# Two encoder layers in split float32: the gate and half of the output projection multiply high and low parts as one product of 512 columns

## The chip, the cores and the metric

The kernel runs on one core of a Trainium2 chip. TensorE (PE) multiplies, VectorE (DVE), ScalarE (ACT) and GpSimd (POOL) work beside it, SyncE (SP) issues loads. Times are device microseconds of the whole execution, the median of the runs. A profile is one execution recorded by the hardware; its span runs from the first to the last instruction of the program.

## The reference

Two layers over 256 positions of width 2048. Each layer is RMSNorm, an input projection into a convolution group and an attention group with their gates, an output projection with residual, and a gated embedding:

```python
for i in range(DEPTH):                       # 2
    hn = _rmsnorm(h, norm_g[i])
    u = hn @ w_in[i]                         # 2048 -> 5632 columns
    ...                                      # ya: convolution group, yb: attention group, 1024 each
    h = h + jnp.concatenate([ya, yb], axis=-1) @ w_out[i]     # 2048 -> 2048
    e = _rmsnorm(p[i] @ w_pe[i], pe_g[i])
    h = h + e * jax.nn.sigmoid(h @ w_pg[i])                   # 2048 -> 2048
return _rmsnorm(h, final_g)
```

Everything is float32.

## The kernel before

Activations lie with the width on the 128 partitions and the 256 positions along the free dimension, so a 2048-wide operand is 16 rows of tiles, 128 x 256 each. A float32 product is made of three products in a reduced type (float32r): each operand is split into a high part (a cast) and a low part (the value less its high part), and `mm3` (lines 398 to 403) sums high x high (L401), high weights x low operand (L402) and low weights x high operand (L403) in one PSUM bank. One such group of three, for one tile of 128 rows, is called a **step** here.

**Weights** come as a stream of **halves** of 128 x 1024, which is eight tiles of 128 x 128, in the order of their use; 156 halves are one layer. Two halves are one load of 1 MB on SP's queue, three loads deep. `split` (L163) casts a half to its high part on ACT (L168) and subtracts on DVE for the low part (L171), into one of five buffers `w`. `get` emits, before the products of half h, the split of half h + 4. The cast of that half waits until TensorE is through with half h - 1, which had the buffer. Engines work strictly in the order in which the code emits, each in its own queue.

**Operands** are tiles of 128 x 2 x 8 x 256: first the eight high parts of eight rows, then the eight low parts. `bigt` makes them: `hg` (the normed input), `ya` and `yb` (what the two groups hand to the output projection), `h1` (the sum after it, the gate's operand).

**The stretch around the change**, with a layer's halves counted from 0:

- Halves 92 to 107: first half of the output projection, over `yb`, summed into `az`. The convolution group's LayerNorm runs beside it on DVE and ACT.
- Halves 108 to 123: its second half, over `ya`. Two output tiles share a PSUM bank `o`; behind a pair stands one add of 512 columns into `az` (DVE, L778), a cast to `h1`'s high part (ACT, L779), and the subtraction for its low part (DVE, L780), which `later` puts behind the next half's products.
- Halves 124 to 155: the gate, two halves to a tile, two tiles to a pair and a bank `g`. The first pair takes rows 0 to 7 of both tiles first and then rows 8 to 15, so that `h1`'s last rows are needed in the third gate half. `gate` does the rest of a pair: sum of `h1`'s parts (DVE, L799), sigmoid (ACT, L801), product and sum (DVE, L803, L804), square (ACT, L391) for the next norm. The last two tiles are single, with 256 columns in `gate`. In the second layer ACT also scales the results (L817). Beside the first 14 gate halves DVE norms the embedding, one L540 to a half.

Of the kernel before, what the change touches and what calls it, by code (L numbers as in the profile page):

```python
# [10 lines left out]
F32 = mybir.dt.float32  # L11
F32R = mybir.dt.float32r
# [5 lines left out]
P = 128  # L18
# [30 lines left out]

NB_FIRST = KT  # L50
NSPL = 5
SHIFT = 16
MAN = 'DVE,PE,Activation'
LY = (2, 2)
ORD = 1
# [74 lines left out]
def trunk_kernel(ctx: ExitStack, tc: tile.TileContext, xT, pT, wst, par, gain, relb, sinkp, onehot, out):  # L130
# [12 lines left out]
    def bigt(name, dt=F32):  # L143

        return big.tile([P, 2, 8, S], dt, tag="big", name=name)

    def halves(t):
        return [t[:, 0], t[:, 1]]

    def bank(name):  # L150
        return ps.tile([P, 2, S], F32, tag="ps", name=name)
# [11 lines left out]
    def split(h):  # L163
        raw = raws[h // 2][:, h % 2, :]
        w = wspl.tile([P, 2 * HALF + 64], F32R, tag="w", name=f"w{h}")
        w = w[:, SHIFT:SHIFT + 2 * HALF].rearrange("p (t n) -> p t n", t=2)
        hi, lo = w[:, 0], w[:, 1]
        nc.scalar.copy(hi, raw)  # L168
        spl[h] = w
        if h not in (4, 5):  # L170
            nc.vector.tensor_sub(lo, raw, hi.bitcast(F32))  # L171

    def first_lo(h):

        w = spl[h]
        nc.vector.tensor_sub(w[:, 1], raws[h // 2][:, h % 2, :], w[:, 0].bitcast(F32))

    def ahead(h):

# [218 lines left out]
    def mm3(o, w, x, start, stop):  # L398


        nc.tensor.matmul(o, w[:, 0], x[:, 0], start=start, stop=False, skip_group_check=True)  # L401
        nc.tensor.matmul(o, w[:, 0], x[:, 1], start=False, stop=False, skip_group_check=True)  # L402
        nc.tensor.matmul(o, w[:, 1], x[:, 0], start=False, stop=stop, skip_group_check=True)  # L403

    class Cursor:
        h = 0
# [1 line left out]
    def step(o, X, start, stop):  # L408

        steps([o], X, [start], stop)  # L410

    def steps(os, X, starts, stop):

        parts = []
        for _ in os:
            name, _, k0, nk = HALVES[Cursor.h % NHALF]
            parts.append(get(Cursor.h).rearrange("p t (k c) -> p t k c", k=nk))
            Cursor.h += 1
        for kk in range(nk):
            k = k0 + kk  # L420
            for o, w, start in zip(os, parts, starts):
                mm3(o, w[:, :, kk, :], X[k // 8][:, :, k % 8, :], start and kk == 0, stop and kk == nk - 1)
# [16 lines left out]
    for l in range(DEPTH):  # L439
# [7 lines left out]
        def operand(k, l=l, h=h, hg=hg):  # L447

            i, kk = k // 8, k % 8
            if kk == 0:  # L450
                hg.append(bigt(f"hg{l}_{i}", F32R))
# [20 lines left out]
        for q in range(4):  # L472
            n = Cursor.h
            Cursor.h += 1
            if l:
                w = get(n).rearrange("p t (j k c) -> p t j k c", j=4, k=2)
            else:
                raw = raws[n // 2][:, n % 2, :].rearrange("p (j k c) -> p j k c", j=4, k=2)
            for jj in range(0, 4, 2):
                j = 4 * q + jj  # L480
                b = bank("e")
                for x in range(2):
                    for k in range(2):
                        if l:
                            mm3(b[:, x, :], w[:, :, jj + x, k, :], pp[:, :, k, :], x == 0 and k == 0, k == 1)
                        else:
                            nc.tensor.matmul(b[:, x, :], raw[:, jj + x, k, :], pf[:, k, :], start=x == 0 and k == 0,
                                             stop=k == 1, skip_group_check=True)
                if l == 0 and j // 2 < 4:
                    for k in (4 * (j // 2), 4 * (j // 2) + 2):  # L490
                        if k < KT - 2:
                            square_acc(hacc, h[k // 8][:, k % 8:k % 8 + 2, :], k == 0, nc.vector)
                    if j // 2 == 3:
                        sq = wk.tile([P, 2, S], F32, name="sq", tag="sq", bufs=3)
                        nc.scalar.activation(sq, h[1][:, 6:8, :], AF.Square)
                        hparts = halves_of(sq) + [fold(hacc)]
                if j // 2 == QQ[l][0]:
                    dg = rstd_col(hparts, D, f"rh{l}")
                    ahead(5 if l == 0 else Cursor.h - 1 - q + 5)
                if j // 2 == QQ[l][1]:  # L500
                    rbs.append(rstd_row(dg, f"rh{l}", copy=False))
                    if l == 0:
                        first_lo(4)
                        operands(0, 1)
                        first_lo(5)
                        subs.pop(0)()
                        operands(2, 1)
                if QQ[l][1] + (l == 0) <= j // 2 <= QQ[l][1] + 1:
                    operands(4 * (j // 2 - QQ[l][1]), 2)
                ecopy.append((j, b))  # L510

                while ecopy and 4 * (l == 0) <= j // 2 < 6:
                    copied(*ecopy.pop(0))
            pump()
# [89 lines left out]
        for q in range(4):  # L604
            n = Cursor.h
            Cursor.h += 1
            w = get(n).rearrange("p t (k c) -> p t k c", k=4)
            for kk in range(4):
                k = 4 * q + kk
                for b in range(2):  # L610
                    mm3(vb[b][:, 0, :], hg[k // 8][:, :, k % 8, b * P:(b + 1) * P], w[:, :, kk, :],
                        k == 0, k == KT - 1)
            pump()
        v = wk.tile([P, 2, W_KV], F32, name=f"v{l}", tag="v", bufs=1)
        for b in range(2):
# [85 lines left out]
        for t in range(0, NCT, 2):  # L701
            b = pair(hg, f"za{l}_{t}")
            if t == NCT - 2:
                finish(l)

                for k in (0, 4):
                    nc.gpsimd.dma_start(a[:, k:k + 4, :], hsrc[:, k:k + 4, :])
                yb = bigt(f"yb{l}", F32R)
# [3 lines left out]
        ya = bigt(f"ya{l}", F32R)  # L712

        def lnorm(l=l, acc=acc, za=za, ya=ya, ysum=ysum, done=done):

# [54 lines left out]
        for j in range(0, KT, 2):  # L770
            d = az[:, j // 8, j % 8:j % 8 + 2, :]
            if j % 8 == 0:
                h1.append(bigt(f"h1{l}_{j // 8}", F32R))
# [4 lines left out]
            nc.vector.tensor_add(d, b, d)  # L778
            nc.scalar.copy(hi, d)  # L779
            sub = lambda d=d, hi=hi, lo=lo: nc.vector.tensor_sub(lo, d, hi.bitcast(F32))  # L780
            if j < KT - 2:
                later(sub)
            else:
                sub()
# [40 lines left out]
        hparts = []  # L825
        for j in range(0, KT - 2, 2):
            if j:
                b = pair(h1, f"g{l}_{j}")
            else:
                b = bank(f"g{l}_{j}")  # L830
                for n in range(2):
                    for x in range(2):
                        step(b[:, x, :], h1, n == 0 and x == 0, n == 1)
            gate(j, b)
            if j == 4 and not last:
                pp = wk.tile([P, 4 * S + 32], F32R, name="pp", tag="qq")
                pp = pp[:, 24:24 + 4 * S].rearrange("p (x k s) -> p x k s", x=2, k=2)
                hilo(pp[:, 0], pp[:, 1], pf)
        for j in range(KT - 2, KT):
            b = bank(f"g{l}_{j}")[:, 0:1, :]  # L840
            for n in range(2):
                step(b[:, 0, :], h1, n == 0, n == 1)
            gate(j, b)
        drain()
        h = e

# [92 lines left out]
```

## Time and profile before

| | us |
|---|---|
| median of 3 runs | 937.89 (937.57 to 939.52) |
| the profiled execution | 937.63 |
| its span | 935.9 |
| weight casts on ACT, 308 | 315.5 busy |
| weight subtractions on DVE, 306 | 374.1 busy |
| adds of 512 behind the second half of the output projection, 16 | 11.0 busy |

The granted TensorE clock is 0.997 of full speed over the span. A row of the groups reads: line, engine, operation, output and inputs by the program's names, shapes, count, then busy time and mean ns of one, then the idle time ahead of them and what ended it. In a timeline the first number is the start in us from the span's start, the second the duration; successive products overlap, so their distance is read from the starts.

### The profile page before, as it was taken

Reading aid. Unit: us, or ns where it says so; the run is one execution under the profiler, and the core shown is the slowest. Engines: PE = TensorE matmul, PEld = TensorE weight load, DVE = VectorE, ACT = ScalarE, POOL = GpSimd, SP = SyncE. Lnnn points to the kernel's source line nnn. Section 1 sums busy time; section 2 is a strip of 40 time slices with the busy share of each in tenths; the row PEclk is TensorE's granted clock in tenths of the full one; section 3 lists DMA queues with packets and bytes.
Section 4 is the critical chain, followed back from the end, with each engine's and each line's share of the span. In section 5 each row is a group of like instructions: output and inputs, shape, how many; then the busy total and the mean of one; then the engine's idle time right before and its main releaser. Section 6 shows DMA issues by size and latency. Waiting matters only on the chain.

```text
span 935.9 us, 19124 instructions
## 1 busy us (share of the span) xinstructions
PE 923.6 (99%) x7968; PEld 910.3 (97%) x7968; DVE 767.6 (82%) x1282; ACT 548.9 (59%) x830; POOL 82.4 (9%) x79
## 2 busy tenths in 40 slices
PE   8999999999999999999999999999999999999995
PEld 7999999999999999999999999999999999999995
DVE  4999999998887686786679999999888877777663
ACT  4655454788874555554467444569788546445551
POOL 0022001010000000011102100000100000000111
PEclk9999999999999999999999999999999999999998
DMA  8674556555547456556656556465555564655532
GB/s 301 232 251 158 203 180 239 184 198 187 183 162 257 164 203 218 182 181 238 210 183 203 180 203 226 171 214 196 187 169 181 182 208 154 244 183 181 202 111 91
DMA packets 29011, 182.55 MB, mean 195 GB/s; under 512 B 3595, under 2 KB 4156, under 8 KB 9084
## 3 DMA queue, kind: packets, MB, share of 16 engines
q1 hardware_dynamic: 24284, 165.70, 50.6%
q0 software_dynamic: 3344, 12.88, 4.3%
q10 hardware_dynamic: 1296, 2.75, 0.8%
q8 instruction: 62, 1.02, 0.4%
q14 instruction: 25, 0.20, 0.1%
HBM read 177.09 MB, written 4.23 MB: 194 GB/s over the span
## 4 chain that ended last, share of the span: by engine, by line
PE 95%; DVE 2%; DMA 1%; ACT 1%; issue 0%; POOL 0%; ACTq 0%; DVEq 0%
PE ag L401 6%; PE ag L402 6%; PE ag L403 6%; PE o L401 6%; PE o L402 6%; PE o L403 6%; PE g L403 6%; PE g L402 6%; PE g L401 6%; PE za L401 3%; PE za L403 3%; PE za L402 3%; PE zb L403 3%; PE zb L401 3%; PE zb L402 3%; PE q L401 3%
## 5 line engine op out<-in xcount | busy, mean ns | idle before, releaser
L171 DVE TENSOR_TENSOR w<-raw,w 128x1024 fp32r<-128x1024 f32 x306 | 374.1, 1231 | 100.0 <-ACT w L168 99.0
L168 ACT CAST w<-raw 128x1024 fp32r<-128x1024 f32 x308 | 315.5, 1046 | 160.1 <-PE ag L403 44.0
L565 DVE SCALAR_TENSOR_TENSOR cz<-az,pars,cz 128x241 f32<-128x241 f32 (+11 forms) x480 | 216.7, 500 | 1.0
L401 PE MATMUL ag<-hg,w 128*128 128x256 f32 x512 | 142.2, 278 | 0.0
L402 PE MATMUL ag<-hg,w 128*128 128x256 f32 x512 | 141.8, 277 | 0.0
L403 PE MATMUL ag<-hg,w 128*128 128x256 f32 x512 | 141.8, 277 | 0.0
L403 PE MATMUL g<-h,w 128*128 128x256 f32 x512 | 141.3, 276 | 0.0
L401 PE MATMUL g<-h,w 128*128 128x256 f32 x512 | 141.3, 276 | 0.0
L402 PE MATMUL g<-h,w 128*128 128x256 f32 x512 | 141.3, 276 | 0.0
L401 PEld LDWEIGHTS ag<-hg,w 128*128 128x128 f32 x512 | 96.1, 188 | 0.9 <-ACT w L168 0.8
L402 PEld LDWEIGHTS ag<-hg,w 128*128 128x128 f32 x512 | 96.4, 188 | 0.1
L403 PEld LDWEIGHTS ag<-hg,w 128*128 128x128 f32 x512 | 96.1, 188 | 0.0
L401 PEld LDWEIGHTS g<-h,w 128*128 128x128 f32 x512 | 96.1, 188 | 0.0
L402 PEld LDWEIGHTS g<-h,w 128*128 128x128 f32 x512 | 96.1, 188 | 0.0
L403 PEld LDWEIGHTS g<-h,w 128*128 128x128 f32 x512 | 96.1, 188 | 0.0
L401 PE MATMUL za<-hg,w 128*128 128x256 f32 x256 | 71.7, 280 | 0.0
L401 PE MATMUL o<-yb,w 128*128 128x256 f32 x256 | 71.4, 279 | 0.0
L401 PE MATMUL q<-hg,w 128*128 128x256 f32 x256 | 71.4, 279 | 0.0
L401 PE MATMUL zb<-hg,w 128*128 128x256 f32 x256 | 71.3, 279 | 0.0
L403 PE MATMUL zb<-hg,w 128*128 128x256 f32 x256 | 71.0, 277 | 0.0
L402 PE MATMUL zb<-hg,w 128*128 128x256 f32 x256 | 71.0, 277 | 0.0
L403 PE MATMUL za<-hg,w 128*128 128x256 f32 x256 | 71.0, 277 | 0.0
(227 smaller groups left out, 2264.0 us busy)
## 6 DMA issues: line engine op xcount, KB each, us to landing
raw<-in_wst SPq DMA_DIRECT2D x153, 1024.0 KB, 4.9
bias<-fscr POOLq DMA_DIRECT2D x16, 384.0 KB, 3.9
raw<-in_wst SPq DMA_DIRECT2D x4, 512.0 KB, 8.1
az<-in_xT POOLq DMA_DIRECT2D x4, 512.0 KB, 5.6
hscr<-e POOLq DMA_DIRECT2D x2, 1024.0 KB, 5.7
az<-hscr POOLq DMA_DIRECT2D x4, 512.0 KB, 6.0
x<-in_xT SPq DMA_DIRECT2D x3, 512.0 KB, 8.4
out_t<-og ACTq DMA_DIRECT2D x4, 256.0 KB, 3.0
```

The source lines that it names most:

```text
L168: nc.scalar.copy(hi, raw)
L171: nc.vector.tensor_sub(lo, raw, hi.bitcast(F32))
L401: nc.tensor.matmul(o, w[:, 0], x[:, 0], start=start, stop=False, skip_group_check=True)
L402: nc.tensor.matmul(o, w[:, 0], x[:, 1], start=False, stop=False, skip_group_check=True)
L403: nc.tensor.matmul(o, w[:, 1], x[:, 0], start=False, stop=stop, skip_group_check=True)
L565: nc.vector.scalar_tensor_tensor(acc[:, t, lo_:hi_], a[:, t, lo_ + s:hi_ + s], w(k), acc[:, t, lo_:hi_], ALU.mult, ALU.add)
```

## The change

Operands lie as 128 x 8 x 2 x 256 now (`operand_tile`): the high and the low part of a row side by side, 512 columns in one piece; views keep the old index order. In the weight buffers the low part begins 32 elements further on (20 from half 108 on), and `split` hands out the two parts instead of one tile.

`mm3` has two forms. Where the output has three dimensions, high weights multiply the 512 columns of high and low operand in one product, and low weights multiply the high part into the second 256 columns. A whole PSUM bank then belongs to one tile, and its two halves are summed afterwards. All other uses keep three products (`prod3`). The wide form is used in the second half of the output projection, and in the gate but for the last tile of the second layer.

In the output projection each tile has its own bank and two adds of 256 columns into `az`. In the gate `merge` copies each tile's second 256 columns to SBUF on ACT and adds the first 256 on DVE; the sigmoid reads that sum.

```diff
+    def operand_tile(name):
+        t = big.tile([P, 8, 2, S], F32R, tag="big", name=name)
+        return t.rearrange("p k t s -> p t k s")
...
     def mm3(o, w, x, start, stop):
-        nc.tensor.matmul(o, w[:, 0], x[:, 0], start=start, stop=False, skip_group_check=True)
-        nc.tensor.matmul(o, w[:, 0], x[:, 1], start=False, stop=False, skip_group_check=True)
-        nc.tensor.matmul(o, w[:, 1], x[:, 0], start=False, stop=stop, skip_group_check=True)
+        if len(o.shape) == 3:
+            nc.tensor.matmul(o, w[0], x, start=start, stop=False, skip_group_check=True)
+            nc.tensor.matmul(o[:, 1], w[1], x[:, 0], start=False, stop=stop, skip_group_check=True)
+            return
+        prod3(o, w, parts_of(x), start, stop)
...
+    def merge(bs):
+        t = wk.tile([P, 2, S], F32, name="hl", tag="ptt")[:, 0:len(bs), :]
+        for x, b in enumerate(bs):
+            nc.scalar.copy(t[:, x, :], b[:, 1, :])
+            nc.vector.tensor_add(t[:, x, :], b[:, 0, :], t[:, x, :])
+        return t
...
+    def wide(X, name):
+        b = bank(name)
+        step(b, X, True, False)
+        step(b, X, False, True)
+        return b
...
-            b = bank(f"o{l}_{j}")
             for x in range(2):
-                step(b[:, x, :], Y, x == 0, True)
-            nc.vector.tensor_add(d, b, d)
+                b = bank(f"o{l}_{j + x}")
+                step(b, Y, True, True)
+                for y in range(2):
+                    nc.vector.tensor_add(d[:, x, :], b[:, y, :], d[:, x, :])
             nc.scalar.copy(hi, d)
...
             if j:
-                b = pair(h1, f"g{l}_{j}")
+                bs = [wide(h1, f"g{l}_{j + x}") for x in range(2)]
...
-            gate(j, b)
+            gate(j, merge(bs))
```

On TensorE a step of the second half of the output projection was, and is now (`ya` the operand, `w` the weights, `o` the bank; the last number is the columns streamed):

```order
L401 MATMUL o_0_4092<-ya_3556,w_3978 128x256
L402 MATMUL o_0_4092<-ya_3556,w_3978 128x256
L403 MATMUL o_0_4092<-ya_3556,w_3978 128x256
...
L414 MATMUL o_0_4092<-ya_3556,w_3978 128x512
L415 MATMUL o_0_4092<-ya_3556,w_3978 128x256
```

Three products have become two. On DVE the order there was as follows, from the first pair on (L171 subtracts for a weight half, L778 adds the bank to `az`, L780 makes a low part of `h1`):

```order
L171 TENSOR_TENSOR w_4095<-raw_3976,w_4095 128x1024
L171 TENSOR_TENSOR w_4122<-raw_3976,w_4122 128x1024
L778 TENSOR_TENSOR az_257<-o_0_4092,az_257 128x512
L171 TENSOR_TENSOR w_4154<-raw_4034,w_4154 128x1024
L780 TENSOR_TENSOR h_0_4091<-az_257,h_0_4091 128x512
L171 TENSOR_TENSOR w_4182<-raw_4034,w_4182 128x1024
L778 TENSOR_TENSOR az_257<-o_2_4151,az_257 128x512
```

and is now (L183 is the weight subtraction, L818 the adds, L820 the low part):

```order
L183 TENSOR_TENSOR w_4095<-raw_3976,w_4095 128x1024
L818 TENSOR_TENSOR az_257<-o_0_4092,az_257 128x256 x2
L183 TENSOR_TENSOR w_4117<-raw_3976,w_4117 128x1024
L818 TENSOR_TENSOR az_257<-o_1_4116,az_257 128x256 x2
L183 TENSOR_TENSOR w_4142<-raw_4034,w_4142 128x1024
L820 TENSOR_TENSOR h_0_4091<-az_257,h_0_4091 128x2x256
L818 TENSOR_TENSOR az_257<-o_2_4139,az_257 128x256 x2
L183 TENSOR_TENSOR w_4165<-raw_4034,w_4165 128x1024
L818 TENSOR_TENSOR az_257<-o_3_4164,az_257 128x256 x2
```

Two adds stand behind every half now, and the weight subtraction of a pair's second half stands behind the first half's adds. On ACT the second pair of the gate, which had the sigmoid (L801) right behind the casts, has two copies ahead of it (casts are L180, copies L432, sigmoid L841, square L403 now):

```order
L180 CAST w_4626<-raw_4526 128x1024
L180 CAST w_4646<-raw_4526 128x1024
L432 COPY hl<-g_2_4580 128x256
L432 COPY hl<-g_3_4623 128x256
L841 ACTIVATE sg<-hl 128x512
L403 ACTIVATE sq<-e_131 128x512
L180 CAST w_4683<-raw_4581 128x1024
```

The casts of the next four halves stand behind the square, as before; the sigmoid reads the merged sum.

More of the change, by code (lines that the diff above doesn't have):

```diff
@@ L51, with shift @@
 NSPL = 5
-SHIFT = 16
+LONG = 108
+def shift(h):
+    return 16, 4 if h % NHALF >= LONG else 16
 MAN = 'DVE,PE,Activation'
@@ L165, in split @@
         w = wspl.tile([P, 2 * HALF + 64], F32R, tag="w", name=f"w{h}")
-        w = w[:, SHIFT:SHIFT + 2 * HALF].rearrange("p (t n) -> p t n", t=2)
-        hi, lo = w[:, 0], w[:, 1]
+        a, b = shift(h)
+        hi, lo = w[:, a:a + HALF], w[:, HALF + 32 + b:2 * HALF + 32 + b]
         nc.scalar.copy(hi, raw)
-        spl[h] = w
+        spl[h] = (hi, lo)
         if h not in (4, 5):
@@ L173, in first_lo @@
     def first_lo(h):
-        w = spl[h]
-        nc.vector.tensor_sub(w[:, 1], raws[h // 2][:, h % 2, :], w[:, 0].bitcast(F32))
+        hi, lo = spl[h]
+        nc.vector.tensor_sub(lo, raws[h // 2][:, h % 2, :], hi.bitcast(F32))
     def ahead(h):
@@ L398, in mm3, with prod3, parts_of @@
     def mm3(o, w, x, start, stop):
-        nc.tensor.matmul(o, w[:, 0], x[:, 0], start=start, stop=False, skip_group_check=True)
-        nc.tensor.matmul(o, w[:, 0], x[:, 1], start=False, stop=False, skip_group_check=True)
-        nc.tensor.matmul(o, w[:, 1], x[:, 0], start=False, stop=stop, skip_group_check=True)
+        if len(o.shape) == 3:
[3 more added lines that the diff above has]
+        prod3(o, w, parts_of(x), start, stop)
+    def prod3(o, w, x, start, stop):
+        nc.tensor.matmul(o, w[0], x[0], start=start, stop=False, skip_group_check=True)
+        nc.tensor.matmul(o, w[0], x[1], start=False, stop=False, skip_group_check=True)
+        nc.tensor.matmul(o, w[1], x[0], start=False, stop=stop, skip_group_check=True)
+    def parts_of(x):
+        return [x[:, 0], x[:, 1]]
+    def merge(bs):
[4 more added lines that the diff above has]
+        return t
     class Cursor:
@@ L416, in steps @@
             name, _, k0, nk = HALVES[Cursor.h % NHALF]
-            parts.append(get(Cursor.h).rearrange("p t (k c) -> p t k c", k=nk))
+            parts.append(get(Cursor.h))
             Cursor.h += 1
@@ L421, in steps @@
             for o, w, start in zip(os, parts, starts):
-                mm3(o, w[:, :, kk, :], X[k // 8][:, :, k % 8, :], start and kk == 0, stop and kk == nk - 1)
+                mm3(o, [y[:, kk * P:(kk + 1) * P] for y in w], X[k // 8][:, :, k % 8, :],
+                    start and kk == 0, stop and kk == nk - 1)
         for _ in os:
@@ L450, in operand @@
             if kk == 0:
[L451 removed]
+                hg.append(operand_tile(f"hg{l}_{i}"))
             rb = rbs[0]
@@ L475, in trunk_kernel @@
             if l:
-                w = get(n).rearrange("p t (j k c) -> p t j k c", j=4, k=2)
+                w = [y.rearrange("p (j k c) -> p j k c", j=4, k=2) for y in get(n)]
             else:
@@ L484, in trunk_kernel @@
                         if l:
-                            mm3(b[:, x, :], w[:, :, jj + x, k, :], pp[:, :, k, :], x == 0 and k == 0, k == 1)
+                            mm3(b[:, x, :], [y[:, jj + x, k, :] for y in w], pp[:, :, k, :], x == 0 and k == 0, k == 1)
                         else:
@@ L606, in trunk_kernel @@
             Cursor.h += 1
-            w = get(n).rearrange("p t (k c) -> p t k c", k=4)
+            w = get(n)
             for kk in range(4):
@@ L610, in trunk_kernel @@
                 for b in range(2):
-                    mm3(vb[b][:, 0, :], hg[k // 8][:, :, k % 8, b * P:(b + 1) * P], w[:, :, kk, :],
-                        k == 0, k == KT - 1)
+                    prod3(vb[b][:, 0, :], parts_of(hg[k // 8][:, :, k % 8, b * P:(b + 1) * P]),
+                          [y[:, kk * W_KV:(kk + 1) * W_KV] for y in w], k == 0, k == KT - 1)
             pump()
@@ L827, in trunk_kernel @@
             if j:
-                b = pair(h1, f"g{l}_{j}")
+                bs = [wide(h1, f"g{l}_{j + x}") for x in range(2)]
             else:
-                b = bank(f"g{l}_{j}")
+                bs = [bank(f"g{l}_{x}") for x in range(2)]
                 for n in range(2):
-                    for x in range(2):
-                        step(b[:, x, :], h1, n == 0 and x == 0, n == 1)
-            gate(j, b)
+                    for b in bs:
+                        step(b, h1, n == 0, n == 1)
+            gate(j, merge(bs))
             if j == 4 and not last:
@@ L839, in trunk_kernel @@
         for j in range(KT - 2, KT):
[L840 to L843, printed above, removed]
+            if last and j == KT - 1:
+                b = bank(f"g{l}_{j}")[:, 0:1, :]
+                for n in range(2):
+                    step(b[:, 0, :], h1, n == 0, n == 1)
+                gate(j, b)
+            else:
+                gate(j, merge([wide(h1, f"g{l}_{j}")]))
         drain()
```

6 lines of the change are left out of this document (3 added, 3 removed).

## The prediction

> **What bounds the kernel now.** I read the page's busy shares first, then the chain that ended last.
>
> ```profile
> span 935.9 us, 19124 instructions
> PE 923.6 (99%) x7968; PEld 910.3 (97%) x7968; DVE 767.6 (82%) x1282; ACT 548.9 (59%) x830; POOL 82.4 (9%) x79
> PE 95%; DVE 2%; DMA 1%; ACT 1%; issue 0%; POOL 0%; ACTq 0%; DVEq 0%
> ```
>
> TensorE is the chain, so a nanosecond off a product counts as often as the product stands there, as long as nothing else becomes late. Next the timeline of PE in the gate stage, eight steps apart (a step is the three products of one 128-row tile):
>
> ```profile
> 386.50 0.28 PE L401 MATMUL g<-h,w 128*128 128x256 f32 x1
> ...
> 388.54 0.28 PE L401 MATMUL g<-h,w 128*128 128x256 f32 x1
> ...
> 389.22 0.28 PE L401 MATMUL g<-h,w 128*128 128x256 f32 x1
> ```
>
> (389.22 - 386.50) / 8 = 0.340 us a step, 113.3 ns a product. Is that the stream of 256 columns or the load of 128 weights? Two other groups separate them: products that stream one column, and plain float32 products of 256 columns, which the trace counts as two passes.
>
> ```profile
> 17.23 0.58 PE L354 MATMUL rh0c<-ones,fold 128*128 128x1 f32 x4
> 17.68 1.97 PE L487 MATMUL e<-p,raw 128*128 128x256 f32 x8
> 20.21 3.46 PE e L487 x16
> ```
>
> One column still costs (17.68 - 17.23) / 4 = 112 ns, which can only be the weight load. A pass of the float32 product takes 3.46 / 16 = 216 ns with its load inside. So a load of about 112 ns sets the 113.3, and a long stream hides a load.
>
> **The change on TensorE.** A wide step is one product of 512 columns and one of 256, in place of three of 256. Per layer it reaches the second half of the output projection (halves 108 to 123 of the layer's weights, 128 steps) and the gate (halves 124 to 155, 256 steps), without the last gate tile of layer two: 128 + 256 + 128 + 240 = 752 steps. The trace has no 512-column product of this type. Bounds: two streams as now, 226.7 ns (saves nothing), and the 216 ns of the row in which a stream hides its load; I know no reason for less. I take 216, the nearest row that is not limited by a load. The third product still covers the next load, 113.3. Step: 329.3 ns instead of 340, and 752 x 10.7 ns = **8.0 us** off TensorE.
>
> The Trainium skill, page "TensorE: Matmul & The Clock Gate", section "Back-to-back issue gap", gives N / 2.4 + 2.5 ns for a warm product alone: 109.2 ns at 256 columns, 215.8 at 512. By it the pair would save 2.5 ns and the sum would be 1.9 us; the trace's 113.3 disagrees at 256, and no run here shows 512.
>
> **What the change puts on VectorE in the output projection.** There the loop of the two other engines is nearly as long as TensorE's. Timelines of DVE and ACT, one pair of output tiles:
>
> ```profile
> 347.80 1.22 DVE L171 TENSOR_TENSOR w<-raw,w 128x1024 fp32r<-128x1024 f32 x1
> 348.93 0.68 DVE L778 TENSOR_TENSOR az<-o,az 128x512 f32<-128x512 f32 x1
> 351.25 1.23 DVE L171 TENSOR_TENSOR w<-raw,w 128x1024 fp32r<-128x1024 f32 x1 [1.64 <-ACT w L168]
> 352.39 0.69 DVE L780 TENSOR_TENSOR h<-az,h 128x512 fp32r<-128x512 f32 x1
> 353.00 1.22 DVE L171 TENSOR_TENSOR w<-raw,w 128x1024 fp32r<-128x1024 f32 x1
> 354.13 0.69 DVE L778 TENSOR_TENSOR az<-o,az 128x512 f32<-128x512 f32 x1
> ...
> 349.65 0.62 ACT L779 CAST h<-az 128x512 fp32r<-128x512 f32 x1 [2.64 <-DVE az L778]
> 350.17 1.05 ACT L168 CAST w<-raw 128x1024 fp32r<-128x1024 f32 x1
> ```
>
> It is a closed loop: add (0.72 to the copy's start), high copy h (0.52), cast of the next half's weights (1.08 to its subtraction), subtraction (1.14), low part of h (0.61), subtraction (1.13), next add: 5.20 us, under TensorE's 16 x 0.340 = 5.44 for the pair. The change replaces the one add of 512 by four of 256, two behind each half, the second reading what the first wrote. Their price:
>
> ```profile
> 464.18 0.41 DVE L803 TENSOR_TENSOR e<-e,sg 128x256 f32<-128x256 f32 x1
> 464.63 0.42 DVE L804 TENSOR_TENSOR e<-e,hs 128x256 f32<-128x256 f32 x1
> 464.97 0.42 DVE L379 TENSOR_TENSOR fold<-hacc 128x256 f32<-128x256 f32 x1
> 518.90 0.41 DVE L575 TENSOR_TENSOR az<-ag,u 128x256 f32<-128x256 f32 x1
> 519.24 1.21 DVE L171 TENSOR_TENSOR w<-raw,w 128x1024 fp32r<-128x1024 f32 x1
> ```
>
> A successor that needs the result starts 0.45 later (L803 to L804), one that doesn't 0.34 later (L804 to L379; L575, which reads PSUM, to L171). New loop: 0.52 + 1.08 + 1.14 + 0.61 + (0.45 + 0.34) + 1.13 + (0.45 + 0.42 + 0.03) = **6.16 us**, against a wide pair of 16 x 0.3293 = 5.27. VectorE falls behind by 0.9 us per pair, eight pairs long. Where it ends:
>
> ```profile
> 337.54 0.28 PE L401 MATMUL o<-ya,w 128*128 128x256 f32 x1
> 341.46 2.35 DVE L171 TENSOR_TENSOR w<-raw,w 128x1024 fp32r<-128x1024 f32 x2
> 344.45 0.62 ACT L779 CAST h<-az 128x512 fp32r<-128x512 f32 x1 [2.94 <-DVE az L778]
> ```
>
> The first high copy moves from 344.45 to 341.46 + 1.14 + 0.79 + 1.14 + 0.90 = 345.43. The eighth starts at 345.43 + 7 x 6.16 = 388.55, the last low part of h 0.65 later, ready at 389.9. TensorE wants it for rows 14 and 15 of the third gate half (half 126): 337.54 + 18 x 8 x 0.3293 + 6 x 0.3293 = 386.9. So TensorE, which had no wait there, waits **3.0 us**. Before, it reached that step at 388.54 (row above); now 389.9, 1.4 late. Layer two has the same stretch with the same distances:
>
> ```profile
> 791.81 0.28 PE L401 MATMUL o<-ya,w 128*128 128x256 f32 x1
> ...
> 798.73 0.62 ACT L779 CAST h<-az 128x512 fp32r<-128x512 f32 x1 [2.94 <-DVE az L778]
> ```
>
> 798.73 - 791.81 = 6.92, in layer one 344.45 - 337.54 = 6.91: 1.4 late again. Behind this wait stands the whole gate; the 128 wide steps of each projection gain nothing. Each first add waits for its half's products; queued behind it on DVE is the subtraction for the half five on, and on that the load that refills its buffer:
>
> ```profile
> raw<-in_wst SPq DMA_DIRECT2D x153, 1024.0 KB, 4.9
> ```
>
> It lands in 4.9 us, and between a buffer's last subtraction and the next cast from it lie four halves, two loops or 12 us, so the loads stay hidden even when VectorE is late.
>
> **The gate.** Behind the wait 234 wide steps remain in layer one and 218 in layer two: 452 x 10.7 = 4.8 us back. New here, per pair of tiles, are two copies on ACT and two adds on DVE, and the sigmoid behind them. What follows a gate in the ACT queue is the weight cast for four halves on:
>
> ```profile
> 391.70 0.48 DVE L540 SCALAR_TENSOR_TENSOR e<-e,pars,re0rb 128x256 f32<-128x256 f32 x1
> 392.10 0.69 DVE L799 TENSOR_TENSOR hs<-h 128x512 f32<-128x512 f32 x1
> ...
> 403.02 0.60 ACT L801 ACTIVATE sg<-g 128x512 f32<-128x512 f32 x1 [1.61 <-PE g L403]
> 405.11 0.64 ACT L391 ACTIVATE sq<-e 128x512 f32<-128x512 f32 x1 [1.49 <-DVE e L804]
> ...
> 859.38 0.64 ACT L391 ACTIVATE sq<-e 128x512 f32<-128x512 f32 x1 [1.48 <-DVE e L804]
> 859.91 0.89 ACT L817 ACTIVATE og<-e,gains 128x256 f32<-128x256 f32 x2
> 860.72 1.98 ACT L168 CAST w<-raw 128x1024 fp32r<-128x1024 f32 x2
> ```
>
> Loop while VectorE is late: four subtractions of 1.14 and four L540 of 0.40 (6.2), two adds (0.34 + 0.42 to the sigmoid), sigmoid to square 405.11 - 403.02 = 2.09, square 0.54 and cast 1.08: 10.6 us against 32 x 0.3293 = 10.54. In layer one about even, so no new wait. In layer two the L817 pair lies between square and cast (860.72 - 859.91 = 0.81): 11.4, VectorE loses 0.85 per pair until L540 ends after three and a half pairs. The spare it starts from: the weights of half 128 come behind the last low part (389.2 + 0.61), two L540 (0.79) and their own subtraction (1.22), at 391.8; TensorE, past its wait at 389.9, gets there ten steps later, at 393.2. So 1.4 us are used up after two pairs, and the other one and a half cost TensorE some **1.2 us** more.
>
> **Sum.** 2 x 1.4 - 4.8 + 1.2 = -0.8 (instead of -8.0). The profiled execution took 937.63 (span 935.9 and 1.7 around it), 0.03% under the median of 937.89. Forecast **936.8**.
>
> At nothing I cost the last gate tile, which stays narrow, so the end of the kernel is as it was. Layer one's last tile is wide, and its copy and add (0.8) delay the square that the next layer's norm sums:
>
> ```profile
> 469.60 0.42 DVE L804 TENSOR_TENSOR e<-e,hs 128x256 f32<-128x256 f32 x1
> ...
> 472.55 0.58 PE L354 MATMUL rh1c<-ones,sq 128*128 128x1 f32 x4
> ```
>
> The sum is done at 470.0, the square 0.45 later, and TensorE comes to it at 472.55 behind the next layer's first products: 2.1 us of cover. Were it gone, the price would be the 0.8. At nothing also the new places of low parts for the products that stay narrow, which are the least known. Windows of PE with counts:
>
> ```profile
> 30.00:60.00 30.00, 30.00 (x252) 1.00 0.64 222
> 60.00:118.00 58.00, 58.00 (x514) 1.00 0.57 192
> ```
>
> 119 ns a product first and 113 then, at one clock. I count 240 steps on this slower beat, 13.3 ns each: 3.2 us to gain. All 1,470 other narrow steps on it would cost 19.6. It starts and ends at waits and float32 products, which all remain, so I take 0.
>
> **Rivals.**
> - *VectorE is not late, or less:* the second add follows like the others (0.34). The loop is 5.94, the first high copy 0.2 earlier, and the last low part ready near 388.1, where TensorE stood at 388.5 before: 2 x (-0.4) - 4.8 + 1.2 = -4.4, 933.2. With no waits at all 929.6. For it: a chain of many terms of which each may be 2% long. Against: L803 to L804, and that the loop of before comes out at the traced 5.20. The Trainium skill, "VectorE: DVE Perf Modes", section "The DRAIN you can't avoid", says that a semaphore after every operation cost nothing extra, by which this rival would hold; the 0.45 against 0.34 above disagrees. Chance 0.27.
> - *The wide product saves nothing:* 512 columns take twice 113.3, or the wide step meets a slower beat of its own. TensorE then comes to rows 14 and 15 at 388.54 as before, and the low part still at 389.9: 1.4 later in each layer, nothing back, 940.4, slower. It decides from a step of about 338 ns on (2.8 - 452 x 2.0 ns = +1.9 us). The page on TensorE named above is a case of it: with its 337.5 ns 2.8 - 452 x 2.5 ns = +1.7 us, 939.3. For it: nothing here streams 512 columns of this type. Against: 216. Chance 0.20.
> - *The narrow beat moves* with the new places: 3 us either way, 0.03 each.
> - That the change isn't there: the PE rows of the changed program have the 128x512 products.
>
> **How the numbers follow.** Forecast 0.47 (its own range 935.5 to 939). What can be told from no change is 0.2%, 1.9 us. Faster: 0.27 + 0.03 = 0.30. Slower: 0.20 + 0.03 = 0.23. Same: 0.47. The range 932.5 to 940.6 leaves out the cases without waits and the far slow ones.
>
> **What would show it.** Wide steps 0.329 apart in the projection. DVE's pairs there 6.1 to 6.2 us apart, not 5.3. One PE wait of about 3 us in the third gate half of each layer, released by the low part of h on DVE; in layer two further waits on weights. No PE wait, or a step near 0.340, makes the forecast wrong.

## The result, and the profile after

The changed kernel takes 944.85 us (943.21 to 945.09, 4 runs) against 937.88 for the kernel before (937.57 to 939.52, 4 runs): ratio 1.0067, 95% interval 1.0055 to 1.008. It is slower by 7.0 us, where 936.8 was forecast and 940.6 was the upper end of the range.

The page of the changed kernel, first the span, the busy time of each engine and the chain that ended last:

```profile
span 943.0 us, 17728 instructions
...
PE 928.5 (98%) x7216; PEld 883.0 (94%) x7216; DVE 790.9 (84%) x1361; ACT 555.3 (59%) x861; POOL 82.1 (9%) x79
...
PE 82%; DVE 11%; ACT 3%; issue 1%; DMA 1%; POOL 0%; ACTq 0%; DVEq 0%
```

752 products fewer, and TensorE is busy 4.9 us longer (928.5 against 923.6). VectorE has a tenth of the chain now. The groups of the wide products (L414 streams 512 columns, L415 the 256 of the low weights; last the idle time ahead of them and what ended it):

```profile
L414 PE MATMUL g<-h,w 128*128 128x512 f32 x496 | 173.6, 395 | 2.7 <-DVE h L820 2.7
...
L415 PE MATMUL g<-h,w 128*128 128x256 f32 x496 | 138.5, 279 | 0.0
...
L414 PE MATMUL o<-ya,w 128*128 128x512 f32 x256 | 87.1, 389 | 0.0
```

The same product takes 389 ns in the projection (`o`) and 395 in the gate (`g`). What that means for the step is in the timeline of PE (start, duration), first in the projection, then around the wait and behind it:

```profile
337.18 0.39 PE L414 MATMUL o<-ya,w 128*128 128x512 f32 x1
337.40 0.28 PE L415 MATMUL o<-ya,w 128*128 128x256 f32 x1
...
339.90 0.39 PE L414 MATMUL o<-ya,w 128*128 128x512 f32 x1
...
387.50 0.39 PE L414 MATMUL g<-h,w 128*128 128x512 f32 x1
387.72 0.28 PE L415 MATMUL g<-h,w 128*128 128x256 f32 x1
389.37 0.51 PE L414 MATMUL g<-h,w 128*128 128x512 f32 x1 [1.37 <-DVE h L820]
389.71 0.28 PE L415 MATMUL g<-h,w 128*128 128x256 f32 x1
389.83 0.39 PE L414 MATMUL g<-h,w 128*128 128x512 f32 x1
...
391.23 0.39 PE L414 MATMUL g<-h,w 128*128 128x512 f32 x1
...
394.03 0.39 PE L414 MATMUL g<-h,w 128*128 128x512 f32 x1
```

Eight steps apart, 339.90 - 337.18 = 2.72: **340 ns a step, what three products of 256 took** (in the prediction's rows of before, 386.50 - 337.54 = 48.96 for the 144 steps from the projection's start into the gate, 340 each). The wide step saves nothing. Behind the wait it is worse: 394.03 - 391.23 = 2.80, **350 ns**, and that holds to the end of the gate in both layers. The wait stands where it was forecast. It costs 389.37 - 387.50 - 0.34 = 1.53, and 0.12 in the step behind it (389.83 - 389.37 = 0.46 instead of 0.34): 1.65 per layer.

So the 7.1 us between the two spans are two waits (3.3), and 29 halves of slower gate per layer (2 x 232 steps x 10 ns = 4.6); the remaining -0.8 lies in the narrow stages and the start of the program. It isn't shown to come from the change: in thirteen profiles whose code is the same up to there, half 92 of layer one begins between 291.34 us (this profile) and 292.91, in the profile of before at 292.12.

The loop on ACT and VectorE at the end of the projection (ACT's high copies of h, then DVE's adds, L818, and the last low part of h, L820):

```profile
381.80 0.62 ACT L819 CAST h<-az 128x512 fp32r<-128x512 f32 x1 [3.66 <-DVE az L818]
...
387.98 0.62 ACT L819 CAST h<-az 128x512 fp32r<-128x512 f32 x1 [3.66 <-DVE az L818]
```

```profile
387.06 0.88 DVE L818 TENSOR_TENSOR az<-o,az 128x256 f32<-128x256 f32 x2
388.62 0.69 DVE L820 TENSOR_TENSOR h<-az,h 128x512 fp32r<-128x512 f32 x1 [0.68 <-ACT h L819]
```

387.98 - 381.80 = 6.18 us for a pair; 6.16 was forecast. Two dependent adds take 0.88 together, which is 0.45 + 0.42, as the prediction had it. The last low part ends at 388.62 + 0.69 = 389.31, and TensorE goes on at 389.37.

### The profile page after: what moved, and what is told of

It is laid out like the page before. It is cut to its first block, busy times and chain, and to the rows that moved or that the text cites. A ratio compares the mean times of both kernels' runs of the same rounds, so it can differ in the third digit from the quotient of the medians.

```text
span 943.0 us, 17728 instructions
## 1 busy us (share of the span) xinstructions
PE 928.5 (98%) x7216; PEld 883.0 (94%) x7216; DVE 790.9 (84%) x1361; ACT 555.3 (59%) x861; POOL 82.1 (9%) x79
## 3 DMA queue, kind: packets, MB, share of 16 engines
q10 hardware_dynamic: 1296, 2.75, 0.8%
## 4 chain that ended last, share of the span: by engine, by line
PE 82%; DVE 11%; ACT 3%; issue 1%; DMA 1%; POOL 0%; ACTq 0%; DVEq 0%
PE g L414 11%; PE ag L421 6%; PE ag L423 6%; PE ag L422 6%; PE g L415 6%; DVE w L183 5%; PE o L421 3%; PE za L421 3%; PE o L422 3%; PE za L423 3%; PE za L422 3%; PE o L423 3%; PE zb L421 2%; PE q L421 2%; PE zb L423 2%; PE q L423 2%
## 5 line engine op out<-in xcount | busy, mean ns | idle before, releaser
L183 DVE TENSOR_TENSOR w<-raw,w 128x1024 fp32r<-128x1024 f32 x306 | 373.8, 1232 | 88.3 <-ACT w L180 85.1
L180 ACT CAST w<-raw 128x1024 fp32r<-128x1024 f32 x308 | 311.8, 1045 | 125.8 <-PE ag L423 42.2
L414 PE MATMUL g<-h,w 128*128 128x512 f32 x496 | 173.6, 395 | 2.7 <-DVE h L820 2.7
L415 PE MATMUL g<-h,w 128*128 128x256 f32 x496 | 138.5, 279 | 0.0
L414 PEld LDWEIGHTS g<-h,w 128*128 128x128 f32 x496 | 93.1, 188 | 24.5 <-DVE h L820 3.4
L415 PEld LDWEIGHTS g<-h,w 128*128 128x128 f32 x496 | 94.1, 190 | 0.0
L414 PE MATMUL o<-ya,w 128*128 128x512 f32 x256 | 87.1, 389 | 0.0
L421 PE MATMUL o<-yb,w 128*128 128x256 f32 x256 | 71.5, 279 | 0.0
L421 PE MATMUL q<-hg,w 128*128 128x256 f32 x256 | 71.3, 279 | 0.0
L421 PE MATMUL zb<-hg,w 128*128 128x256 f32 x256 | 71.1, 278 | 0.0
L422 PE MATMUL o<-yb,w 128*128 128x256 f32 x256 | 70.9, 277 | 0.0
L423 PE MATMUL zb<-hg,w 128*128 128x256 f32 x256 | 70.8, 277 | 0.0
L423 PE MATMUL q<-hg,w 128*128 128x256 f32 x256 | 70.8, 277 | 0.0
```

The lines of the kernel that those rows point to most:

```text
L414: nc.tensor.matmul(o, w[0], x, start=start, stop=False, skip_group_check=True)
L415: nc.tensor.matmul(o[:, 1], w[1], x[:, 0], start=False, stop=stop, skip_group_check=True)
L421: nc.tensor.matmul(o, w[0], x[0], start=start, stop=False, skip_group_check=True)
L422: nc.tensor.matmul(o, w[0], x[1], start=False, stop=False, skip_group_check=True)
L423: nc.tensor.matmul(o, w[1], x[0], start=False, stop=stop, skip_group_check=True)
```

## Experiments

Two things had to be explained: why 512 columns save nothing, and why the gate has a beat of 350 when the projection, with the same products, has 340. In the expectations "4", "16", "0" and "8" are places of the low weights in their buffer. By the distance between a weight's high and low part they are 1044 elements ("4", the changed kernel from half 108 on), 1056 ("16", its other halves), 1040 ("0") and 1048 ("8"); before it was 1024. The high part lies at element 16 of its buffer in every run, so "distance" stands for the place of the low part as well; the runs can't tell the two apart. **Beat** is the time of a step, read as above from PE's starts eight steps apart. The ratios are to runs of the kernel before on the same chip (its medians there lie between 937.88 and 938.74).

| run | projection, halves 108 to 123: form, distance, beat | gate: form, distance, beat | median us | ratio (95%) |
|---|---|---|---|---|
| before | narrow 1024, 340 | narrow 1024, 340 | 937.88 | |
| changed kernel | wide 1044, 340 | wide 1044, 350 behind a wait | 944.85 | 1.0067 (1.0055 to 1.008) |
| e1 | narrow 1044, 353 | wide 1044, 350, no wait | 945.44 | 1.0079 (1.0064 to 1.0094) |
| e2 | wide 1044, 340 | narrow 1044, 353 | 947.36 | 1.0095 (1.008 to 1.0111) |
| e3 | narrow 1044, 353 | narrow 1044, 353 | 948.72 | 1.0112 (1.0095 to 1.0129) |
| e4 | wide 1044, 340 | wide 1044, 350 behind a wait | 947.29 | 1.0099 (1.0084 to 1.0114) |
| e5 | wide 1056, 353 | wide 1056, 353 | 947.56 | 1.0095 (1.008 to 1.011) |
| e6 | narrow 1056, 340 | narrow 1056, 340 | 937.10 | 0.9985 (0.9976 to 0.9995) |
| e7 | wide 1044, 340 | wide 1044, 350 behind a wait | 945.45 | 1.007 (1.0053 to 1.0087) |
| e9 | wide 1044, 340 | wide 1044, 340, then 350 | 942.29 | 1.0042 (1.0026 to 1.0059) |
| e10 | narrow 1056, 340 | wide 1044, 340 throughout | 937.47 | 0.9995 (0.9985 to 1.0004) |
| e11 | wide 1024, 353 | wide 1024, 353 | 948.62 | 1.011 (1.0095 to 1.0125) |
| e12 | narrow 1056, 340 | wide 1044, 350 behind a wait | 955.30 | 1.0164 (1.0128 to 1.02) |
| e13 | narrow 1056, 340 | narrow 1056, 340 behind a wait | 949.30 | 1.0119 (1.0104 to 1.0135) |
| e14 | wide 1040, 350 | wide 1040, 350 | 945.39 | 1.0076 (1.0056 to 1.0096) |
| e15 | wide 1048, 353 | wide 1048, 353 | 947.37 | 1.0097 (1.0077 to 1.0117) |

### One part of the change at a time: e1 to e4

**e1** takes the wide form back in the projection alone:

```diff
+            b = bank(f"o{l}_{j}")
             for x in range(2):
-                b = bank(f"o{l}_{j + x}")
-                step(b, Y, True, True)
-                for y in range(2):
-                    nc.vector.tensor_add(d[:, x, :], b[:, y, :], d[:, x, :])
+                step(b[:, x, :], Y, x == 0, True)
+            nc.vector.tensor_add(d, b, d)
```

> Second half of the output projection narrow again (one bank and one add of 512 per pair), gate wide, new operand layout. Two theories for the gate's beat of 0.350 us a step. Restart: TensorE takes the slower beat when it resumes behind its wait for the low part of h; here the loop of DVE and ACT is 5.2 us a pair again, so no wait, the gate runs at 0.340 and the time is that of the layout alone, about 937. Gate: the beat belongs to the gate's own wide products; then 60 gate halves at 2.80 instead of 2.72 us, about 941.8.

**e2** takes it back in the gate alone, and **e3** in both, so that only the new layout of operands and weights is left:

```diff
-                bs = [wide(h1, f"g{l}_{j + x}") for x in range(2)]
+                b = pair(h1, f"g{l}_{j}")
...
-                    for b in bs:
-                        step(b, h1, n == 0, n == 1)
-            gate(j, merge(bs))
+                    for x in range(2):
+                        step(b[:, x, :], h1, n == 0 and x == 0, n == 1)
+            gate(j, b)
```

> Second half of the output projection wide, gate narrow (the low weights of halves 108 and on keep their place 20 elements further). The wait of 1.66 us per layer stays under both theories. Restart: the narrow gate takes its slower beat behind it (0.353, the 118 ns a product seen elsewhere): 937 + 3.3 + about 6.3 = 946.5. Gate: a narrow gate keeps 0.340, 937 + 3.3 = 940.3.

> All products narrow, with the new operand layout and the new places of the low weights. The changed kernel's narrow stages were 0.7 us ahead in layer one and 0.26 in layer two, so 936.9, same as before. If the layout itself costs something in the gate, its steps are over 0.340 and the time is above 938.

**e4** puts two small float32 products behind each of the halves 126 and 127:

```diff
+    def settle():
+        sb = bank("settle")
+        for b in range(2):
+            nc.tensor.matmul(sb[:, 1, b:b + 1], ones, ones[:, 0:1], start=True, stop=True, skip_group_check=True)
```

> The changed kernel with two small float32 products (one column, ones) behind each of the two gate halves that follow or hold the wait, four a layer, about 0.5 us a half, 2 us in all. Restart: they end the slower beat as float32 products do elsewhere, the gate falls to 0.340 a step, 944.85 + 2.0 - 4.7 = 942.2. Gate: 0.350 stays, 946.9.

Measured: e3 missed its expectation of 936.9 by 11.8 us. With no wide product at all the kernel is slower than the changed one, 948.72. The gate of e3 in PE's timeline, eight steps apart:

```profile
399.89 0.28 PE L421 MATMUL g<-h,w 128*128 128x256 f32 x1
...
402.72 0.28 PE L421 MATMUL g<-h,w 128*128 128x256 f32 x1
```

2.83 / 8 = 354 ns. So the step's time hangs on where the low weights lie: narrow steps with the low part 1044 behind the high one take 353 ns. e1 and e2 fit: each has 353 where it is narrow. That puts e1 (945.44) above both of its expectations, and it makes e2's nearness to 946.5 luck: its gate is at 353 from its first half on, ahead of the wait. e1 has no wait, and yet its gate is at 350:

```profile
L414 PE MATMUL g<-h,w 128*128 128x512 f32 x496 | 173.7, 395 | 0.0
```

That spoke against the wait as the cause of the slow gate, but e1's gate also begins behind a stretch at 353. In e4 the gate is back at 350 two halves behind the small products: they do not set the beat right.

### The distance, the layout and the stream: e5 to e8

**e5** is the changed kernel with distance 1056 everywhere, **e6** is e3 with it:

```diff
-    return 16, 4 if h % NHALF >= LONG else 16
+    return 16, 16
```

> The changed kernel with the low weights of halves 108 and on 32 elements further like all others, not 20 (one number). The layout-only run had the slower beat in both late stages without any wait, so the restart theory is out. Place: the 20 elements make the beat (another offset between high and low weights); then the gate is at 0.340 a step, and 944.85 - 4.7 = 940.1, with the wait of 1.66 per layer kept. Operand: the beat comes with the new layout of the operand; then nothing changes, 944.9.

> All products narrow, new operand layout, all low weights 32 elements further. Place: the late stages fall from 0.353 to 0.340, the layout-only time of 948.7 falls by 4 x 0.33 x ... = 10.2 us to 938.5 or lower (936.9 by the narrow stages). Operand: 948.7 stays.

**e7** is the changed kernel with the operands as they were, the 512 columns as two pieces of 256:

```diff
-        t = big.tile([P, 8, 2, S], F32R, tag="big", name=name)
-        return t.rearrange("p k t s -> p t k s")
+        return big.tile([P, 2, 8, S], F32R, tag="big", name=name)
```

> The changed kernel with the operands laid out as before (eight high parts, then eight low parts); the wide product reads its 512 columns as two pieces of 256. Weights placed as in the changed kernel. Operand: the gate falls to 0.340, 940.1, if two pieces stream like one. Place: 0.350 stays, 944.9. Two pieces slower than one would show in the projection, at over 0.340 a step.

**e8** is the kernel before with rows of 48 equal products behind its end, to measure the stream by itself:

```diff
+    def probe(name, wcols, n, src, half):
+        o = bank(name).rearrange("p a b -> p (a b)")
+        for i in range(48):
+            w = src[:, half + i % 4 * P:half + i % 4 * P + wcols]
+            nc.tensor.matmul(o[0:wcols, 0:n], w, src[:, 0:n], start=True, stop=True, skip_group_check=True)
```

> The kernel before with nine rows of 48 independent products behind its end, on finished data: float32r with 128 weights by 512, 384, 256 and 128 columns, 64 weights by 256 and 512, and bfloat16 with 128 by 512 and 256 and 64 by 256; their sums are thrown away. Stream theory (the columns of this type come at 0.443 ns each): 512 at 226.7, 384 at 170, 256 at 113.3 with 128 and with 64 weights alike, bfloat16 512 near 216. Load theory (the weight load sets the distance): 256 falls below 113 with 64 weights, 512 comes near 216. The time is longer than before by some 60 us and means nothing.

Measured: e6 against e3 changes nothing but the distance, and the gate falls from 354 to 2.72 / 8 = 340 ns:

```profile
399.86 0.28 PE L421 MATMUL g<-h,w 128*128 128x256 f32 x1
...
402.58 0.28 PE L421 MATMUL g<-h,w 128*128 128x256 f32 x1
```

The wide step wants the opposite: in e5, at 1056, where 940.1 or 944.9 was expected and 947.56 came, it takes 353 in projection and gate, from the first wide half on, although the stretch before it runs at 340:

```profile
L414 PE MATMUL o<-ya,w 128*128 128x512 f32 x256 | 90.5, 397 | 0.0
```

(The mean duration of a 512-column product goes with the beat: 389 ns at 340, 395 at 350, 397 at 353.) e7 repeats the changed kernel, its beats and its wait: the layout of the operands plays no part in the beats. e8, groups by shape, is about the stream (the number behind `*` is the columns of weights loaded; `p` is float32r, `h` bfloat16):

```profile
L874 PE MATMUL p64x<-probe 128*64 128x512 f32 x48 | 11.2, 392 | 0.0
L874 PE MATMUL p128x<-probe 128*128 128x512 f32 x48 | 11.1, 390 | 0.0
L874 PE MATMUL h128x<-probeh 128*128 128x512 bf16 x48 | 10.5, 379 | 0.0
...
L874 PE MATMUL p128x<-probe 128*128 128x256 f32 x48 | 5.9, 283 | 0.0
L874 PE MATMUL p64x<-probe 128*64 128x256 f32 x48 | 5.6, 276 | 0.0
L874 PE MATMUL p128x<-probe 128*128 128x128 f32 x48 | 5.5, 273 | 0.0
...
L874 PE MATMUL h128x<-probeh 128*128 128x256 bf16 x48 | 5.4, 273 | 0.0
```

Busy time less one duration, over 47, is the distance of two products: 228 ns for 512 columns of float32r, 230 with half the weights, 215 in bfloat16; at 256 columns 120, 113 with half the weights, and 109 in bfloat16; at 128 columns 111. The first few of the 512 are slower; settled, they are (3.56 - 0.39) / 14 = 226.4 apart (the row's rounding leaves about 1 ns open):

```profile
949.62 3.56 PE L874 MATMUL p128x<-probe 128*128 128x512 f32 x15
```

Three things follow. **512 columns of float32r take 226.4 ns, twice 113, and half the weights don't shorten that** (230). At 256 columns half the weights leave 113 as well, so the stream alone needs the 113.3 of the kernel before. Second, the load is nearly as long: the 111 at 128 columns fits the load of 112 ns that the prediction read from one column (no row with half the weights separates load and stream at 128). Load and stream were equal within 2 ns, so hiding a load freed nothing. Third, beside 256 columns a full load can cost 7 ns more (120), which half a load does not. VectorE, ScalarE and GpSimd are busy for 0.00 us in these rows, so no other engine's work is needed for it. It points to loads that hinder the stream beside them as the source of the slow beats, though half a load did not help the 512 columns. Why the place of the weights decides it isn't shown.

By the Trainium skill, "TensorE: Matmul & The Clock Gate", section "Back-to-back issue gap", a warm product alone takes N / 2.4 + 2.5 ns, 215.8 and 109.2: the bfloat16 rows agree with it (215 and 109), the float32r rows don't (226.4 and 113).

### Does the wait bring the slow beat on? e9 to e13

**e9** gives TensorE the rows 0 to 7 of four gate tiles first, not of two, so that it asks for the last low part of h 10.9 us later:

```diff
     for k0 in (0, 8):
-        for j in range(2):
+        for j in range(4):
             out.append(("w_pg", tile_cols(j), k0, 8))
...
+                bs = [bank(f"g{l}_{x}") for x in range(4)]
+                for b in bs:
+                    step(b, h1, True, False)
+                for x, b in enumerate(bs):
+                    step(b, h1, False, True)
+                    if x == 1:
+                        gate(0, merge(bs[0:2]))
+                bs, j = bs[2:4], 2
```

> The changed kernel, with the rows 0 to 7 of the first four gate tiles (not two) ahead of any rows 8 to 15, so that TensorE has 21 us instead of 10.9 before it asks for the last low part of h. Both theories: the wait of 1.67 us per layer goes. If the wait (a restart of the stream) locks in the slower beat, the gate comes back to 340 ns a step and the time is 944.9 - 3.3 - 4.7 = 936.9. If the wide step in the gate has the slower beat of its own, the gate stays at 350 and the time is about 944.9 - 3.3 = 941.5.

**e10** is e1 with the distance 1044 from half 124 on only, so that the narrow projection is at 1056:

```diff
-LONG = 108
+LONG = 124
```

> The projection as before (narrow, low weights at 16), the gate wide with its low weights at 4 from its first half (124) on. No wait on h, and TensorE enters the gate from a beat of 340. If a wide gate is slow only when it is entered slow or from a wait, the gate is at 340 and the time that of the kernel in which all is narrow at 16, 937.1. If it is slow of its own, 350 and 937.1 + 2 x 2.6 = 942.3.

**e11** is the changed kernel with the distance of before everywhere (`return 16, -16` in `shift`):

> The changed kernel, with every low part of the weights where it was before (1024 elements behind the high part, not 1056 or 1044). If the distance alone decides and the distance of before is a good one for wide steps too, projection and gate are at 340 and only the waits are left: about 937.5 + 3.3 = 940.8. If wide steps want another distance than narrow ones, they are at 350 to 353 as with the low part at 16, and the time is 945 to 948. The narrow stages go back to the beats of before in both (some 0.9 us more than in the changed kernel).

Measured: e10 answers the first half of the question. No wait, a way in at 340, and the wide gate keeps 340 through all its halves in both layers (402.49 - 399.77 = 2.72):

```profile
399.77 0.39 PE L414 MATMUL g<-h,w 128*128 128x512 f32 x1
...
402.49 0.39 PE L414 MATMUL g<-h,w 128*128 128x512 f32 x1
```

So 350 is not the wide gate's own. e9 (942.29) came out above both of its expectations, 936.9 and 941.5: the wait on h is gone, but both gates fall to 350 later, and layer two's meets waits for weights. In layer two the gate runs at 340 for twelve halves (but for half 128, see below), then comes a wait for weights, and then it is at 350:

```profile
851.72 0.39 PE L414 MATMUL g<-h,w 128*128 128x512 f32 x1
...
854.44 0.39 PE L414 MATMUL g<-h,w 128*128 128x512 f32 x1
...
869.74 0.39 PE L414 MATMUL g<-h,w 128*128 128x512 f32 x1
870.86 0.39 PE L415 MATMUL g<-h,w 128*128 128x256 f32 x1 [0.73 <-DVE w L183]
...
873.19 0.39 PE L414 MATMUL g<-h,w 128*128 128x512 f32 x1
...
875.99 0.39 PE L414 MATMUL g<-h,w 128*128 128x512 f32 x1
```

854.44 - 851.72 = 2.72 ahead of it, 875.99 - 873.19 = 2.80 behind it. In layer one, however, e9 slips to 350 at half 128 with no wait in the trace. In layer two the same half takes 2.75 us instead of 2.72, and the next is at 340 again. So a wait is not needed for the slower beat, and a small disturbance can pass. e11 shows that 1024, good for narrow steps, gives wide ones 353.

**e12** puts nothing but a wait into e10; **e13** puts the same into e6, where all is narrow. The last low part of h takes two extra copies by a DMA queue:

```diff
             if j < KT - 2:
                 later(sub)
             else:
-                sub()
+                t = [wk.tile([P, 2, S], F32R, name="late", tag="ptt") for _ in range(2)]
+                nc.vector.tensor_sub(t[0], d, hi.bitcast(F32))
+                nc.gpsimd.dma_start(t[1], t[0])
+                nc.gpsimd.dma_start(lo, t[1])
```

> The kernel with a wide gate behind a narrow projection (937.5, gate at 340 ns), with one thing added: the last low part of h goes through two copies by the DMA queue of GpSimd, so that it is ready some 4 to 5 us later and TensorE waits for it in half 126, as in the changed kernel. If a wait alone throws wide steps into the slower beat, the gate is at 350 from there on: 937.5 + 2 x (about 1.5 + 2.3) = 945. If it takes more than a wait, the gate comes back to 340 and the time is 937.5 + 2 x 1.5 = 940.5.

> The same wait put into the kernel in which all steps are narrow with the low weights at 16 (937.1, gate at 340). If only wide steps stay slow, the gate comes back to 340: 937.1 + 2 x 1.5 = 940.1. If any step that starts from a wait stays on the slower beat, the gate is at 353: 937.1 + 2 x (1.5 + 3.1) = 946.3.

Measured: the wait is longer than meant, 4.4 and 4.2 us, which puts both times above what was expected. e12, PE's timeline at the wait and some halves later:

```profile
393.76 0.77 PE L414 MATMUL g<-h,w 128*128 128x512 f32 x1 [4.38 <-DMA h<-late]
...
399.89 0.40 PE L414 MATMUL g<-h,w 128*128 128x512 f32 x1
...
402.69 0.40 PE L414 MATMUL g<-h,w 128*128 128x512 f32 x1
```

e13, the same:

```profile
392.64 0.39 PE L422 MATMUL g<-h,w 128*128 128x256 f32 x1 [4.17 <-DMA h<-late]
...
400.06 0.28 PE L421 MATMUL g<-h,w 128*128 128x256 f32 x1
...
402.78 0.28 PE L421 MATMUL g<-h,w 128*128 128x256 f32 x1
```

The wide gate comes back at 2.80 / 8 = 350 ns and stays there; the narrow one comes back at 2.72 / 8 = 340. e10 and e12 differ in the two copies alone, and what these bring to TensorE is the wait: **in these profiles a wait moves wide steps at 1044 from 340 to 350 up to the gate's end, in both layers, and narrow steps at 1056 recover.** Form and place change together here, since narrow steps at 1044 and wide ones at 1056 are slow without a wait. One of e12's four executions took 949.62, the others 954.79 to 956.55; it has no profile, so whether its gate stayed at 350 isn't known. e12's wait is long enough for the granted clock to fall for a while (below); those of the changed kernel (1.37 us) and of e9 (0.73) are not, and they end at 350 too.

### Two more places: e14 and e15

In the changed kernel, `return 16, 0 if ...` and `return 16, 8 if ...` in place of the 4:

> The changed kernel with the low weights of the halves from 108 on at 0 instead of 4. If the place decides whether a wide beat recovers from a wait, another place may give 340 in projection and gate: 944.9 - 4.7 = 940.2. If 0 behaves as 16 does, both are at 353: 947.6. If as 4 does, 944.9.

> As with the low weights at 0, with 8 instead: 940.2 where the beat recovers from the wait, 944.9 if 8 behaves as 4 does, 947.6 if as 16 does.

Measured: 945.39 and 947.37. At 1040 and 1048 the projection, too, is slow from its first wide half (350 and 353 ns), with the last low part then in time or nearly so. So e14's time is that of "if as 4 does" by luck: a slower projection stands in for the waits. Of the five distances tried, 1024, 1040, 1044, 1048 and 1056, only 1044 ever lets the wide step run at 340, and none does better.

No run with a wide step is faster than before. e6, without one, is: 0.9985 (0.9976 to 0.9995). Of its gain of 0.15%, 1.4 us, the two profiles show 0.8 (span 935.1 against 935.9). Some of it is in narrow stages that meet fewer slow beats: between the last gate product of layer one and half 92 of layer two, 221 products of 256 columns are followed only after 115 to 125 ns, 370 in the kernel before, and the stretch takes 278.13 us instead of 278.41.

## Why the prediction was wrong

**The step that failed is "I take 216, the nearest row that is not limited by a load".** The products of one column showed that a load takes 112 ns; that the load therefore sets the 113.3 did not follow, since a stream of 256 columns can take as long as a load, and does (e8: 113 with half the weights). The row with 216 was a pass of 256 columns of plain float32 and didn't carry over to 512 of float32r: e8 has 226.4 for these. The bound on the other side, "two streams as now, 226.7 ns (saves nothing)", was the right end. Of the 8.0 us nothing came, and the 4.8 that the gate was to give back stayed out.

**The loop on VectorE was right.** Adds, the dependent second add, the loop of a pair (6.16 forecast, 6.18 measured), the place of the wait (rows 14 and 15 of the third gate half), its releaser and the release (389.9 forecast, 389.37 measured) hold. TensorE got there later than forecast, as its steps were 340 and not 329, so the wait is 1.4 us long and not 3.0; lateness against before, which is what counts, is 1.65 per layer instead of 1.4. The rival by which a dependent add costs no more than another one falls with the 0.88 of two adds (0.34 + 0.42 = 0.76 by that rival). That a semaphore after every operation costs nothing extra, as the section "The DRAIN you can't avoid" of the Trainium skill's "VectorE: DVE Perf Modes" has it, doesn't carry over to these two adds. The loop's terms add up to 6.17 rather than 6.16, which changes nothing.

**The gate's beat was the second miss.** "Or the wide step meets a slower beat of its own" stood among the rivals with the price of nothing saved, 940.4. That rival had the right sign and the right two waits (2.8 forecast, 3.3 measured), but no price for a beat above 340. It comes to 4.6 us, and it is not the step's own, since e10 holds 340: a wait brings it on (e12 against e10), a slow way in does too (e1 against e10), and e9's layer one fell into it with neither. The change made both the wait and the step that doesn't recover from it.

**The weight waits in layer two's gate (1.2) did not come.** The likely reason is the beat: at 350 a step TensorE takes 32 x 0.350 = 11.2 us for a pair, about the 11.4 of VectorE's loop while its own work is late. In e9, where the gate is at 340 up to there, two came (0.73, row above, and some 0.3 four halves on); e10, whose projection is narrow, had none at 340. The term itself was added up too low: three and a half pairs at 0.85, less the spare of 1.4, are 1.6.

**The places of the low parts were taken at 0,** as "the least known", with 3 us either way and 0.03 for each side. For the stages that stayed narrow no more than -0.8 showed. What was not seen is that the place and the form belong together: the halves from 108 on had another place, which is a bad one for narrow steps (353, e3) and the only good one for wide ones.

The miss of 8.0 us adds up so: 4.8 (no saving in the gate) + 4.6 (its slower beat) - 1.2 (no weight waits) + 0.5 (longer waits) - 0.8 (narrow stages and start) = 7.9.

## What to carry to other kernels

Before a product is made longer to save loads, find out which of the two sets its pace, with a row in which only one of them changes and in the same type: a price from another type missed here by 10 ns in 226, which was the whole gain. Here load and stream took nearly the same time, so sparing one left the other. A step had more than one steady beat in these runs, and a wait could move it to a slower one that outlasted it by far: 1.65 us of waiting were followed by 2.3 us of slower steps. So read the beat behind each wait, not only the wait.

## What the hardware showed that was not expected

- The time of a step depends on where the low weights lie in SBUF, told here by their distance from the high ones: narrow steps 340 ns at 1024 and 1056 elements and 353 at 1044; wide steps 340 or 350 at 1044, 350 at 1040, 353 at 1024, 1048 and 1056. Which part of the memory makes it so was not found out.
- A wide step at 1044 has two steady beats. What made e9 slip in layer one with no wait, and not in layer two, stays open.
- A wait of 4.4 us costs more than itself. Windows of PE in e12 (the window and its length, busy time and count, granted clock, share of the DMA engines, GB/s):

```profile
389.00:394.00 5.00, 0.62 (x4) 0.96 0.76 246
394.00:397.00 3.00, 3.00 (x10) 0.50 0.00 0
397.00:400.00 3.00, 3.00 (x19) 0.99 0.37 76
```

The clock is granted by half for some 3 us behind it, ten products where nineteen would fit. In the changed kernel, around its wait of 1.37 us, it stays at 1.00:

```profile
387.00:390.00 3.00, 1.63 (x9) 1.00 0.61 169
```

By the Trainium skill, "TensorE: Matmul & The Clock Gate", section "Part 1: The HAM clock gate (the "warmup" mystery)", an idle window of about 3.4 us drops the clock to half; the 4.4 and 1.37 us of these runs agree.
